# First mixer: input transposed raw, 1/rms put on later as a row, low-rank weights loaded early, first embedding product ahead, values by halves of K

## Chip, cores and metric

One core of one Trainium2 chip runs the whole program in one launch. The metric is device time of an execution in microseconds; for the kernel before it is the median of three runs. TensorE (PE) multiplies, VectorE (DVE) and ScalarE (ACT) do elementwise work, GpSimd (POOL) does small powers and issues some loads, SyncE (SP) issues most loads.

## The reference, cut to what matters

The program is two blocks over 256 positions of width 1024. The first block's first layer is the RWKV mixer, followed by a gated per-layer embedding. The rest (a differential attention layer, feed-forward layers, a Mamba mixer, windowed attention) isn't touched but for where some of its constants are loaded.

```python
def rwkv7_mixer(h, mu, w_in, w0, w1, w2, a0, a1, a2, ...):   # h = rms_norm(x, rw_norm)
    dx = token_shift(h) - h
    xm = h[:, :, None, :] + dx[:, :, None, :] * mu[:4]
    r, k, v, gate = einsum('bsgd,dgc->bsgc', xm, w_in)        # four 1024 x 1024 products
    xw, xa = h + dx * mu[4], h + dx * mu[5]
    w_log = -softplus(-(w0 + tanh(xw @ w1) @ w2)) - 0.5       # low rank, 64
    a = sigmoid(a0 + (xa @ a1) @ a2)                          # low rank, 64
    ...                                                       # recurrence over 256 positions, 16 heads
    return (y * silu(gate)) @ w_out

g = sigmoid(rms_norm(h, pe_norm[i]) @ pe_w_gate[i])
h = h + g * (p[i] @ pe_w_proj[i])                             # i = 0, 1; p[i] is 256 x 256
```

## The kernel before

Weights come from DRAM in f32 tiles of 512 KB or 256 KB (`wload`: tile wr). ScalarE copies a tile to its high part wh, VectorE subtracts to get the low part wl, and each product of f32 accuracy is three matmuls: high by high, high by low, low by high. The activations are split in the same way. Tiles of 128 x 512 come from one pool (`s`, 36 of them); a load into a tile waits until the tile's last reader is done.

The first stage, `rwkv`, runs in this order. x (four tiles of 128 x 512) is squared and summed on ScalarE (`rstd`), GpSimd takes the power -1/2, VectorE scales the four tiles (hn), TensorE transposes them in sixteen 128 x 128 pieces, and ScalarE evacuates them with the gain rw_norm as a column into hT. VectorE makes the differences dx between neighbouring positions. `mixf` makes the mixed input of one projection for two of eight K slices (two multiply-adds on VectorE), `mix` splits it. `value(g)`, `gate(g)`, and the k and r products in `pre(g)` are made for four groups g of 256 columns by `linear2_g`, which yields after every half of a weight tile of four K slices. `lora` makes the two low-rank products from the weights wa, and wm, which is wa times the mu column. Its result feeds the second low-rank product in `pre(g)`, with the weights w2 of that group (tile w in the trace), and with that the recurrence begins.

The code builds its steps as generators, and `weave` runs several in turns. The order on each engine is then set by a scheduler, except that instructions given to `late` stay in program order. Engines work strictly in that order. The last `weave` of the stage runs four streams (one per group: `pre`, `scores`, `solve`, `post`), the gates, and, from step 50 on, `ple_proj(0)` and `ple_proj(1)`: each transposes p[i], multiplies it by pe_w_proj[i] in four groups of twelve matmuls, and stores the product to DRAM (pp) for the stage that adds it.

Loads around it: ScalarE's queue carries the constants, rw_norm, rw_mu, and through the stage the rows (`rows`) and w2 weights of each group. SP carries x, the weights and eleven small vectors (`load_vec`) of later stages. GpSimd carries the level masks lev, wa and five column vectors (`mid_cols`).

Of the kernel before, what the change touches and what calls it, by code (L numbers as in the profile page):

```python
# [18 lines left out]
P = 128  # L19
# [122 lines left out]
class Net:  # L142
    def __init__(self, ctx, tc, I, out, cst, dbg=None):
        self.tc, self.nc, self.I, self.out = tc, tc.nc, I, out
        self.dbg = dbg or {}
        nc = tc.nc
        self.V, self.A, self.T, self.G = nc.vector, nc.scalar, nc.tensor, nc.gpsimd
        self.uid, self.at = 0, None
        en = lambda name, bufs, **k: ctx.enter_context(tc.tile_pool(name=name, bufs=bufs, **k))
        self.cp = en("cp", 1)  # L150
        self.wp = en("wp", 1)
        self.sp = en("sp", 36)
        self.mp = en("mp", 4)
# [42 lines left out]
    def tt(self, out, a, b, op):  # L196
        self.V.tensor_tensor(out=out, in0=a, in1=b, op=op)  # L197

    def mul(self, out, a, b):
        self.tt(out, a, b, ALU.mult)  # L200
# [10 lines left out]
    def ts(self, out, a, s1, op0, s2=None, op1=None):  # L211
        if s2 is None:
            self.V.tensor_scalar(out=out, in0=a, scalar1=s1, scalar2=None, op0=op0)
        else:
            self.V.tensor_scalar(out=out, in0=a, scalar1=s1, scalar2=s2, op0=op0, op1=op1)  # L215
# [6 lines left out]
    def act(self, out, a, f=AF.Copy, **k):  # L222
        self.A.activation(out, a, f, **k)  # L223

    def mm(self, out, l, r, start=True, stop=True):
        self.T.matmul(out, l, r, start=start, stop=stop)  # L226
# [22 lines left out]


    def prologue(self, cst):
# [4 lines left out]
        nc.scalar.dma_start(self.cst, cst[:, :C_KEEP])  # L256
# [35 lines left out]
    def load_x(self, tile, early=False):  # L292

        self.H = {(t, f): tile[:, t * 2 + f] for t in range(2) for f in range(2)}
        for (t, f), h in self.H.items():
# [41 lines left out]
    def wload(self, W, k0, kn, n0, nn):  # L337
# [10 lines left out]
        if self.nw <= 3:  # L348
            self.late(ins)
# [203 lines left out]
    def ple_proj(self, i):  # L553
# [4 lines left out]
        self.nc.sync.dma_start(pv, I["p"][i, 0].rearrange("(t p) d -> p t d", p=P))  # L558
# [47 lines left out]
    def rwkv(self, nxt):  # L606
# [21 lines left out]
        self.G.dma_start(lev[:, :7], self.cdram[:, C_LEV:C_LEV + 7 * P].rearrange("p (a b) -> p a b", a=7))  # L628
# [307 lines left out]
        for q, n in enumerate(("rw_w1", "rw_a1")):  # L936
            self.late(self.G.dma_start(wa[:, :, q], I[n][0].rearrange("(k p) n -> p k n", p=P)))
# [5 lines left out]
        weave(chain(*[value(g) for g in range(4)]), chain(lora(), mix(1, *xk), mix(0, *xr)))  # L943
        weave(mix(3, *xg))
        def residual():
# [9 lines left out]
              after(FP, chain(self.ple_proj(0), self.ple_proj(1))), when(done(OP[0]), after(OP[1], chain(take(l0, OP[2]), take(l1, OP[3])))),  # L955
# [4 lines left out]
    def diff(self, nxt):  # L960
# [7 lines left out]
        for j in range(2):  # L968
            self.mul(lt[:, j * 64:(j + 1) * 64], self.vec[f"da_lq{j + 1}"], self.vec[f"da_lk{j + 1}"])
# [121 lines left out]
    def ssm(self, nxt):  # L1091
# [92 lines left out]
        self.act(ar, self.vec["ssm_a_log_2"], AF.Exp)  # L1184
# [27 lines left out]
        self.ts(hD, self.vec["ssm_d_2"], 0.5, ALU.mult)  # L1212
# [3 lines left out]
        self.ts(mneg, self.tri, 1.0, ALU.subtract, -NEG, ALU.mult)  # L1216
# [344 lines left out]
```

## Time and profile before

| | us |
|---|---|
| three runs | 1552.46, 1554.59, 1555.87; median 1554.59 |
| the profiled execution | 1552.2 |
| its span, first to last instruction | 1550.0 |
| TensorE busy | 1499.0 (97%) |
| VectorE busy | 1063.5 (69%) |
| ScalarE busy | 813.6 (52%) |
| chain that ended last, share on TensorE | 85% |

The span is the time from the first instruction to the last; 2.2 us of the execution's own time lie around it. Busy time of TensorE is counted over pipelined matmuls, so a full TensorE may still have small holes. In a timeline row the first number is the start in us, the second the time that the merged instructions took, x the count, and the bracket the idle time ahead with what ended it. Line numbers are those of the kernel before.

### The profile page before, as it was taken

The numbers are of one execution on the slowest core, as the hardware profiler recorded it, in microseconds if no ns is written. First come the engines' busy times: TensorE is split into PE (matmuls) and PEld (weight loads), VectorE is DVE, ScalarE is ACT, GpSimd is POOL, SyncE is SP. The second block draws the span as 40 slices with busy tenths as digits, with TensorE's granted clock in tenths as the row PEclk, the third lists the DMA queues.
The fourth block names the chain that finished last, engine by engine and source line by source line (L and its number), as shares of the span: only waits on it lengthen the run. The fifth ranks groups of instructions, "written<-read, shape, count | busy, mean of one in ns | idle before, by whom it ended". The sixth has DMA issues, their size and how long they took to land.

```text
span 1550.0 us, 25809 instructions
## 1 busy us (share of the span) xinstructions
PE 1499.0 (97%) x10164; PEld 1336.5 (86%) x10164; DVE 1063.5 (69%) x1798; ACT 813.6 (52%) x1374; POOL 76.7 (5%) x79
## 2 busy tenths in 40 slices
PE   4999999999899999999999999999999999999998
PEld 3988998777678999887788899988999987799987
DVE  6887887787487665559888656655756547766563
ACT  3546556555466543447667644444644445754342
POOL 0000001111101000000000000000000002000000
PEclk9999999999999999999999999999999999999999
DMA  7421324657846654664443655474654753355453
GB/s 208 140 80 59 93 83 137 222 179 148 251 156 192 192 166 151 241 196 130 115 135 110 205 173 167 147 249 149 192 189 133 249 189 109 96 177 177 150 204 109
DMA packets 145501, 249.90 MB, mean 161 GB/s; under 512 B 11161, under 2 KB 42921, under 8 KB 145380
## 3 DMA queue, kind: packets, MB, share of 16 engines
q1 hardware_dynamic: 138420, 233.87, 47.2%
q0 software_dynamic: 3200, 10.81, 3.3%
q10 hardware_dynamic: 3760, 3.58, 0.9%
q8 instruction: 80, 1.31, 0.3%
q14 instruction: 41, 0.34, 0.1%
HBM read 242.16 MB, written 6.29 MB: 160 GB/s over the span
## 4 chain that ended last, share of the span: by engine, by line
PE 85%; DVE 6%; DMA 3%; ACT 2%; POOL 2%; issue 1%; ACTq 0%; POOLq 0%; DVEq 0%
PE pl L226 71%; PE ps L226 10%; PE ps L229 3%; DVE wl L197 1%; DMA wr<-in_da_w_in_dram 1%; DVE s L197 1%; DMA wa<-in_rw_a_dram 1%; DVE s L209 1%; ACT wh L223 1%; ACT s L223 1%; POOL m L234 1%; DMA wr<-in_pe_w_gate_dram 0%; POOL m L1382 0%; ACT e L223 0%; DVE ac L209 0%
## 5 line engine op out<-in xcount | busy, mean ns | idle before, releaser
L226 PE MATMUL pl<-wh,s 128*128 128x512 f32 (+1 forms) x2336 | 678.8, 369 | 5.6 <-DVE s L197 2.9
L197 DVE TENSOR_TENSOR wl<-wr,wh 128x1024 fp32r<-128x1024 f32 (+1 forms) x460 | 528.5, 1173 | 120.9 <-ACT wh L223 119.9
L223 ACT ACTIVATE wh<-wr 128x1024 fp32r<-128x1024 f32 (+1 forms) x460 | 450.9, 1012 | 175.4 <-PE pl L226 105.7
L226 PE MATMUL pl<-s,wh 128*128 128x256 f32 x2816 | 509.1, 283 | 0.0
L226 PEld LDWEIGHTS pl<-wh,s 128*128 128x128 f32 x2336 | 422.8, 190 | 74.7 <-DVE s L197 4.0
L226 PEld LDWEIGHTS pl<-s,wh 128*128 128x128 f32 x2816 | 439.4, 192 | 0.2
L226 PE MATMUL pl<-wl,s 128*128 128x512 f32 (+1 forms) x1168 | 430.5, 369 | 2.0 <-DVE wl L197 2.0
L226 PE MATMUL pl<-s,wl 128*128 128x256 f32 x1408 | 398.5, 283 | 0.0
L226 PEld LDWEIGHTS pl<-s,wl 128*128 128x128 f32 x1408 | 270.2, 192 | 0.0
L226 PEld LDWEIGHTS pl<-wl,s 128*128 128x128 f32 x1168 | 221.7, 190 | 35.4 <-DVE wl L197 3.2
L223 ACT ACTIVATE s<-s 128x512 f32<-128x512 f32 (+2 forms) x97 | 61.0, 629 | 209.6 <-DVE s L197 209.4
L197 DVE TENSOR_TENSOR s<-pl,s 128x512 f32<-128x512 f32 x44 | 30.4, 691 | 93.7 <-PE pl L226 93.7
L197 DVE TENSOR_TENSOR s<-pl,R 128x512 f32<-128x512 f32 x44 | 30.3, 691 | 82.8 <-PE pl L226 82.7
L234 POOL TENSOR_TENSOR m<-m,base 128x2 f32<-128x2 f32 (+2 forms) x25 | 25.3, 1016 | 990.7 <-DVE m L215 990.7
L223 ACT ACTIVATE h<-ps 128x512 f16<-128x512 f32 x88 | 48.3, 601 | 29.3 <-PE ps L226 27.3
L223 ACT ACTIVATE s<-ps,base 128x256 fp32r<-128x256 f32 (+1 forms) x104 | 45.7, 471 | 23.6 <-PE ps L229 12.2
L209 DVE SCALAR_TENSOR_TENSOR s<-ps,base,s 128x256 fp32r<-128x256 f32 x96 | 43.7, 479 | 6.8 <-ACT s L223 5.6
L223 ACT ACTIVATE junk<-H 128x512 bf16<-128x512 f32 x40 | 25.1, 627 | 43.6 <-DVE H L209 29.2
L226 PE MATMUL ps<-h,h 128*128 128x128 f16 x544 | 43.8, 220 | 2.8 <-ACT h L223 2.8
L209 DVE SCALAR_TENSOR_TENSOR s<-s,s 128x512 f32<-128x512 f32 x56 | 38.4, 686 | 10.1 <-ACT s L223 9.4
L226 PEld LDWEIGHTS <-h 128*128 128x128 f16 x576 | 35.6, 99 | 10.7 <-issue 6.0
L209 DVE SCALAR_TENSOR_TENSOR H<-pl,m,H 128x512 f32<-128x512 f32 x16 | 12.0, 751 | 47.1 <-PE pl L226 47.1
(231 smaller groups left out, 1290.1 us busy)
## 6 DMA issues: line engine op xcount, KB each, us to landing
wr<-in_ffn_w_dram SPq DMA_DIRECT2D x248, 512.0 KB, 4.9
wr<-in_ssm_w_in_dram SPq DMA_DIRECT2D x40, 512.0 KB, 4.2
wr<-in_rw_w_in_dram SPq DMA_DIRECT2D x32, 512.0 KB, 4.0
wr<-in_da_w_in_dram SPq DMA_DIRECT2D x32, 512.0 KB, 5.1
wr<-in_pe_w_gate_dram SPq DMA_DIRECT2D x16, 512.0 KB, 6.3
wr<-in_ffn_w_dram SPq DMA_DIRECT2D x32, 256.0 KB, 3.0
wr<-in_ssm_w_out_dram SPq DMA_DIRECT2D x16, 512.0 KB, 3.9
wr<-in_rw_w_out_dram SPq DMA_DIRECT2D x8, 512.0 KB
```

The costliest lines, as they stand in the source:

```text
L197: self.V.tensor_tensor(out=out, in0=a, in1=b, op=op)
L209: self.V.scalar_tensor_tensor(out=out, in0=a, scalar=sc, in1=b, op0=op0, op1=op1, **k)
L223: self.A.activation(out, a, f, **k)
L226: self.T.matmul(out, l, r, start=start, stop=stop)
L229: self.T.transpose(out, a, self.ident)
L234: self.G.tensor_tensor(out=out, in0=out, in1=self.mhalf[:, :out.free_size()].rearrange("p (a b) -> p a b", a=out.shape[1]) if len(out.shap ...
```

## The change

In `rwkv` the scaling by 1/rms is gone. TensorE transposes x itself, ScalarE evacuates with the gain as before, and 1/rms is put on afterwards: the two diagonal matrices dg of 1/rms are multiplied by ones, which gives a row R_ of 1/rms over the positions on all partitions, and VectorE multiplies the four hT tiles by it. `ple_proj(0)` leaves the last weave and runs ahead of that: a first part before the low-rank weights, the rest behind the row, its instructions kept in program order (`pinned`). The low-rank weights come from SP, behind x, p[0] and the first embedding weight; x and wa share memory, so the load waits for the last reader of x. The values run as first halves of K for all four groups, then second halves. Half of the constants, the level masks, the vectors, the rows and the w2 weights go to GpSimd's queue.

```diff
     def prologue(self, cst):
-        nc.scalar.dma_start(self.cst, cst[:, :C_KEEP])
+        nc.scalar.dma_start(self.cst[:, :C_CAUS], cst[:, :C_CAUS])
...
+    @contextmanager
+    def pinned(self):
+        self.pin = True
+        yield
+        self.pin = False
+
+    def kept(self, ins):
+
+        if self.pin:
+            self.late(ins)
+        return ins
...
     def load_vec(self):
         for name, o in self.vec.items():
-            self.nc.sync.dma_start(o, self.bc(self.I[name], o.shape[1]))
+            self.late(self.G.dma_start(o, self.bc(self.I[name], o.shape[1])))
...
     def rwkv(self, nxt):
...
         r = self.rstd()
-        hn = {}
-        for f in range(2):
-            for t in range(2):
-                o = hn[t, f] = b()
-                self.ts(o[:], self.H[t, f], r[:, t:t + 1], ALU.mult)
         for k0 in range(0, 8, 2):
             ps = self.pt()
             for j in range(2):
                 for t in range(2):
-                    k = k0 + j
-                    self.tr(ps[:, j * 256 + t * P:j * 256 + (t + 1) * P], hn[t, k // 4][:, (k % 4) * P:(k % 4 + 1) * P])
-            x, d = hT[k0 // 2], dx[k0 // 2]
+                    self.tr(ps[:, j * 256 + t * P:j * 256 + (t + 1) * P], self.hsrc(t, k0 + j))
             for j in range(2):
-                self.act(x[:, j], ps[:, j * 256:(j + 1) * 256], scale=self.col("rw_norm", k0 + j))
+                self.act(hT[k0 // 2][:, j], ps[:, j * 256:(j + 1) * 256], scale=self.col("rw_norm", k0 + j))
+
+        side = self.ple_proj(0)
+        with self.pinned():
+            weave(take(side, 3))
+        for q, n in enumerate(("rw_w1", "rw_a1")):
+            self.late(nc.sync.dma_start(wa[:, :, q], I[n][0].rearrange("(k p) n -> p k n", p=P)))
+        dg, R_ = b((P, 2, P)), b((P, 256))
+        ps = self.pl()
+        for t in range(2):
+            self.ts(dg[:, t], self.ident, r[:, t:t + 1], ALU.mult)
+            self.mm(ps[:, t * P:(t + 1) * P], self.ones, dg[:, t])
+        self.act(R_[:], ps[:, :256])
+        with self.pinned():
+            weave(side)
+        for x, d in zip(hT, dx):
+            self.mul(x[:], x[:], both(R_[:]))
             self.sub(d[:, :, 1:256], x[:, :, 0:255], x[:, :, 1:256])
             self.ts(d[:, :, 0:1], x[:, :, 0:1], -1.0, ALU.mult)
+        self.late(self.G.dma_start(lev[:, :7], self.cdram[:, C_LEV:C_LEV + 7 * P].rearrange("p (a b) -> p a b", a=7)))
+        self.late(self.G.dma_start(self.cst[:, C_CAUS:], self.cdram[:, C_CAUS:C_KEEP]))
...
-                nc.scalar.dma_start(o[:, j], bass.AP(tensor=a.tensor, offset=a.offset + g * 256, ap=[[0, P], [1, 256]]))
+                ins = self.G.dma_start(o[:, j], bass.AP(tensor=a.tensor, offset=a.offset + g * 256, ap=[[0, P], [1, 256]]))
...
-                nc.scalar.dma_start(w2[at:at + 64, q], I[m][0, :, g * 256:(g + 1) * 256])
-                nc.scalar.dma_start(w2[one:one + 1, q], I[c0][:, g * 256:(g + 1) * 256])
+                for d, w in ((w2[at:at + 64, q], I[m][0]), (w2[one:one + 1, q], I[c0])):
+                    ins = self.G.dma_start(d, w[:, g * 256:(g + 1) * 256])
...
-        for q, n in enumerate(("rw_w1", "rw_a1")):
-            self.late(self.G.dma_start(wa[:, :, q], I[n][0].rearrange("(k p) n -> p k n", p=P)))
...
-        weave(chain(*[value(g) for g in range(4)]), chain(lora(), mix(1, *xk), mix(0, *xr)))
+        vs = [value(g) for g in range(4)]
+        weave(chain(*[take(v, 2) for v in vs], *vs), chain(lora(), mix(1, *xk), mix(0, *xr)))
...
-              after(FP, chain(self.ple_proj(0), self.ple_proj(1))), when(done(OP[0]), after(OP[1], chain(take(l0, OP[2]), take(l1, OP[3])))),
+              after(FP, self.ple_proj(1)), when(done(OP[0]), after(OP[1], chain(take(l0, OP[2]), take(l1, OP[3])))),
```

The scheduler then orders each engine anew. On ScalarE, at the head, the evacuations of the transposes (s from ps) stood before among row loads, and mixed inputs (s from b) followed:

```order
L223 ACTIVATE s_97<-ps_126,base_72 128x256 x2
L709 DMA row_115_582<-in_rw_k_a_dram 128x256
L709 DMA row_115_582<-in_rw_r_k_dram 128x256
L709 DMA row_470_2145<-in_rw_ln_b_dram 128x256
L223 ACTIVATE s_98<-ps_135,base_72 128x256 x2
L709 DMA row_470_2145<-in_rw_ln_w_dram 128x256
L223 ACTIVATE s_99<-ps_144,base_72 128x256 x2
L223 ACTIVATE s_100<-ps_153,base_72 128x256 x2
L223 ACTIVATE s_168<-b_165 128x512
```

Now the last evacuation is followed by the split of p (s_152), the weight copies of the embedding product (wh from wr), the row of 1/rms (b_179) and the evacuations of the four product groups (s from pl):

```order
L223 ACTIVATE s_99<-ps_138,base_72 128x256 x2
L223 ACTIVATE s_152<-ps_147 128x512
L223 ACTIVATE wh_159<-wr_158 128x2x256
L223 ACTIVATE b_179<-pl_180 128x256
L223 ACTIVATE s_186<-pl_157 128x512
L223 ACTIVATE wh_191<-wr_190 128x2x256
L223 ACTIVATE s_208<-pl_189 128x512
L223 ACTIVATE wh_213<-wr_212 128x2x256
L223 ACTIVATE s_230<-pl_211 128x512
L223 ACTIVATE wh_235<-wr_234 128x2x256
L223 ACTIVATE wh_304<-wr_303 128x1024
```

An evacuation of one group and the weight copy of the next alternate from group to group. On VectorE, where the values end, the two first low parts of k (wl_624, wl_654) stood before ahead of the last value group's reduction (L692 from pl_469):

```order
L197 TENSOR_TENSOR s_462<-b_458,s_461 128x512
L197 TENSOR_TENSOR s_467<-pl_376,hold_90 128x512
L209 SCALAR_TENSOR_TENSOR b_555<-s_104,base_72,s_100 128x256
L197 TENSOR_TENSOR wl_624<-wr_622,wh_623 128x1024
L197 TENSOR_TENSOR wl_654<-wr_652,wh_653 128x1024
L692 TENSOR_REDUCE hold_90<-pl_469 128x8
L197 TENSOR_TENSOR wl_697<-wr_695,wh_696 128x1024
```

Now, behind the reduction of the last value group pl_430, which is the row just ahead of these, come the gate's mixed inputs (b and s) and only then the first low part of k, wl_729:

```order
L210 SCALAR_TENSOR_TENSOR b_639<-s_100,base_72,s_96 128x256
L214 TENSOR_SCALAR hold_90<-hold_90 128x8
L210 SCALAR_TENSOR_TENSOR b_646<-s_101,base_72,s_97 128x256
L198 TENSOR_TENSOR s_637<-pl_430,hold_90 128x512
L198 TENSOR_TENSOR s_643<-b_639,s_642 128x512
L210 SCALAR_TENSOR_TENSOR b_646<-s_101,base_72,s_97 128x256
L210 SCALAR_TENSOR_TENSOR b_653<-s_102,base_72,s_98 128x256 x2
L198 TENSOR_TENSOR s_650<-b_646,s_649 128x512
L210 SCALAR_TENSOR_TENSOR b_660<-s_103,base_72,s_99 128x256
L198 TENSOR_TENSOR s_657<-b_653,s_656 128x512
L210 SCALAR_TENSOR_TENSOR b_660<-s_103,base_72,s_99 128x256
L198 TENSOR_TENSOR wl_729<-wr_727,wh_728 128x1024
```

The first low part of k moved from ahead of the last value reduction to twelve steps behind it.

## Rows read from the trace of the kernel before

**Rows 1.** The page: busy time by engine, and TensorE's busy tenths in 40 slices.
```profile
PE 1499.0 (97%) x10164; PEld 1336.5 (86%) x10164; DVE 1063.5 (69%) x1798; ACT 813.6 (52%) x1374; POOL 76.7 (5%) x79
...
PE   4999999999899999999999999999999999999998
```

**Rows 2.** Stretches: length, busy time of each engine, granted clock, DMA share, GB/s.
```profile
25.00:30.00 5.00, 3.72 (x15) 3.53 (x16) 5.00 (x13) 1.89 (x3) 0.00 (x0) 0.50 0.39 113
...
30.00:30.50 0.50, 0.50 (x5) 0.50 (x5) 0.50 (x2) 0.00 (x0) 0.00 (x0) 0.85 0.05 13
```

**Rows 3.** Timeline of the head, 0 to 24 us: first matmul, squares, transposes, evacuations.
```profile
7.55 0.33 PE L309 MATMUL ps<-base,s 56*128 56x56 f32 x1 [7.55 <-DMA s<-in_rw_mu_dram]
...
8.24 0.63 ACT L223 ACTIVATE junk<-x 128x512 bf16<-128x512 f32 x1 [2.32 <-DMA x<-in_x_dram]
...
8.99 0.63 ACT L223 ACTIVATE junk<-x 128x512 bf16<-128x512 f32 x1
...
16.01 3.46 PE L229 MATMUL ps<-base,b 128*128 128x128 f32 x15 [0.23 <-DVE b L213]
...
21.54 1.57 ACT L223 ACTIVATE s<-ps,base 128x256 f32<-128x256 f32 x4 [0.18 <-issue]
```

**Rows 4.** Timeline of VectorE: the wait for the low-rank weights.
```profile
23.52 0.69 DVE L197 TENSOR_TENSOR wa<-wa,base 128x512 f32<-128x512 f32 x1 [3.53 <-DMA wa<-in_rw_w_dram]
```

**Rows 5.** Timeline of TensorE: first products, end of the values, start of the recurrence.
```profile
26.28 1.19 PE L226 MATMUL ps<-s,wa 128*128 128x256 f32 x2 [6.80 <-DMA wa<-in_rw_a_dram]
...
27.70 0.41 PE L226 MATMUL pl<-wh,s 128*128 128x256 f32 x1
27.91 0.41 PE L226 MATMUL pl<-wl,s 128*128 128x256 f32 x1
...
33.15 3.19 PE L226 MATMUL ps<-s,wa 128*128 128x256 f32 x14
...
58.24 0.39 PE L226 MATMUL pl<-wl,s 128*128 128x256 f32 x1
...
71.24 1.94 PE L226 MATMUL ps<-w,hold 65*128 65x256 f32 x8
```

**Rows 6.** Groups by shape, 60 to 330 us: busy and mean ns, idle before.
```profile
L223 ACT ACTIVATE s<-pl 128x512 f32<-128x512 f32 x12 | 7.2, 614 | 3.9 <-PE pl L226 3.9
...
L197 DVE TENSOR_TENSOR wl<-wr,wh 128x512 fp32r<-128x512 f32 x8 | 5.4, 684 | 0.0
...
L223 ACT ACTIVATE wh<-wr 128x512 fp32r<-128x512 f32 x8 | 4.9, 647 | 0.0
```

**Rows 7.** Landing times by line: L937 (wa, GpSimd), L346 (weights, SP), L283 (columns, GpSimd).
```profile
DMA to landing us min/median/max: 8.7/9.6/10.4
...
DMA to landing us min/median/max: 3.6/5.9/9.3
...
DMA to landing us min/median/max: 3.2/3.9/4.2
```

**Rows 8.** Timeline of VectorE: mixing steps, a reduction and a split, two low parts.
```profile
35.03 4.84 DVE L209 SCALAR_TENSOR_TENSOR b<-s,base,s 128x256 f32<-128x256 f32 x12
...
52.70 0.68 DVE L692 TENSOR_REDUCE hold<-pl 128x8 f32<-128x512 f32 x1
53.30 0.68 DVE L197 TENSOR_TENSOR s<-b,s 128x512 fp32r<-128x512 f32 x1
...
56.97 2.35 DVE L197 TENSOR_TENSOR wl<-wr,wh 128x1024 fp32r<-128x1024 f32 x2
```

**Rows 9.** One stretch of the recurrence, columns as in rows 2.
```profile
240.00:260.00 20.00, 17.81 (x209) 16.60 (x208) 13.77 (x26) 14.47 (x29) 2.16 (x4) 1.00 0.46 157
```

**Rows 10.** Timeline of ScalarE, 70 to 280 us: first and last of 27 load issues.
```profile
73.22 0.47 ACTq L720 DMA_DIRECT2D w<-in_rw_w_dram  x1
...
265.73 0.80 ACTq L709 DMA_DIRECT2D row<-in_rw_ln_w_dram  x1
```

**Rows 11.** Timeline of GpSimd: the first of the five column loads.
```profile
58.54 0.55 POOL L283 DMA_DIRECT2D s<-in_da_norm_dram  x1 [41.71 <-PE pl L226]
```

More of the change, by code (lines that the diff above doesn't have):

```diff
@@ L196, in tt @@
     def tt(self, out, a, b, op):
-        self.V.tensor_tensor(out=out, in0=a, in1=b, op=op)
+        return self.kept(self.V.tensor_tensor(out=out, in0=a, in1=b, op=op))
     def mul(self, out, a, b):
-        self.tt(out, a, b, ALU.mult)
+        return self.tt(out, a, b, ALU.mult)
     def add(self, out, a, b):
@@ L212, in ts @@
         if s2 is None:
-            self.V.tensor_scalar(out=out, in0=a, scalar1=s1, scalar2=None, op0=op0)
-        else:
-            self.V.tensor_scalar(out=out, in0=a, scalar1=s1, scalar2=s2, op0=op0, op1=op1)
+            return self.V.tensor_scalar(out=out, in0=a, scalar1=s1, scalar2=None, op0=op0)
+        return self.V.tensor_scalar(out=out, in0=a, scalar1=s1, scalar2=s2, op0=op0, op1=op1)
     def masked(self, out, a, b, least, init=3.0e38):
@@ L222, in act @@
     def act(self, out, a, f=AF.Copy, **k):
-        self.A.activation(out, a, f, **k)
+        return self.kept(self.A.activation(out, a, f, **k))
     def mm(self, out, l, r, start=True, stop=True):
-        self.T.matmul(out, l, r, start=start, stop=stop)
+        self.kept(self.T.matmul(out, l, r, start=start, stop=stop))
     def tr(self, out, a):
@@ L248, in late @@
         self.tc.keep_in_program_order(ins)
+    @contextmanager
+    def pinned(self):
+        self.pin = True
+        yield
+        self.pin = False
+    def kept(self, ins):
+        if self.pin:
+            self.late(ins)
+        return ins
     def prologue(self, cst):
@@ L294, in load_x @@
         self.H = {(t, f): tile[:, t * 2 + f] for t in range(2) for f in range(2)}
-        for (t, f), h in self.H.items():
+        for t, f in ((0, 0), (1, 0), (0, 1), (1, 1)):
+            h = self.H[t, f]
             ins = self.nc.sync.dma_start(h, self.I["x"][0, t * P:(t + 1) * P, f * 512:(f + 1) * 512])
@@ L347, in wload @@
         self.nw = getattr(self, "nw", 0) + 1
-        if self.nw <= 3:
+        if self.nw <= 7:
             self.late(ins)
@@ L557, in ple_proj @@
         pv = p[:].rearrange("p (t d) -> p t d", t=2)
-        self.nc.sync.dma_start(pv, I["p"][i, 0].rearrange("(t p) d -> p t d", p=P))
+        ins = self.nc.sync.dma_start(pv, I["p"][i, 0].rearrange("(t p) d -> p t d", p=P))
+        if i == 0:
+            self.late(ins)
         outs = [([], [])]
@@ L708, in rows @@
                 a = I[n]
-                nc.scalar.dma_start(o[:, j], bass.AP(tensor=a.tensor, offset=a.offset + g * 256, ap=[[0, P], [1, 256]]))
+                ins = self.G.dma_start(o[:, j], bass.AP(tensor=a.tensor, offset=a.offset + g * 256, ap=[[0, P], [1, 256]]))
+                if g == 0:
+                    self.late(ins)
             return o
@@ L719, in pre @@
                 one = 64 if q == 0 else 63
-                nc.scalar.dma_start(w2[at:at + 64, q], I[m][0, :, g * 256:(g + 1) * 256])
-                nc.scalar.dma_start(w2[one:one + 1, q], I[c0][:, g * 256:(g + 1) * 256])
+                for d, w in ((w2[at:at + 64, q], I[m][0]), (w2[one:one + 1, q], I[c0])):
+                    ins = self.G.dma_start(d, w[:, g * 256:(g + 1) * 256])
+                    if g == 0:
+                        self.late(ins)
             for q, o in enumerate((lw, a)):
@@ L968, in diff @@
         for j in range(2):
[L969 removed]
+            self.late(self.mul(lt[:, j * 64:(j + 1) * 64], self.vec[f"da_lq{j + 1}"], self.vec[f"da_lk{j + 1}"]))
         self.V.tensor_reduce(out=ls[:], in_=lt[:, :128].rearrange("p (a c) -> p a c", a=2), axis=AX.X, op=ALU.add)
@@ L1183, in ssm @@
         ar = cut(32)
-        self.act(ar, self.vec["ssm_a_log_2"], AF.Exp)
+        self.late(self.act(ar, self.vec["ssm_a_log_2"], AF.Exp))
         dta = cut(128).rearrange("p (a b c) -> p a b c", a=2, b=2)
@@ L1211, in ssm @@
         hD = cut(32)
-        self.ts(hD, self.vec["ssm_d_2"], 0.5, ALU.mult)
+        self.late(self.ts(hD, self.vec["ssm_d_2"], 0.5, ALU.mult))
         sb = self.m([P, 8, P], BF16, "sb", 1)
@@ L1215, in ssm @@
         self.late(self.V.tensor_copy(idb, self.ident))
-        self.ts(mneg, self.tri, 1.0, ALU.subtract, -NEG, ALU.mult)
+        self.late(self.ts(mneg, self.tri, 1.0, ALU.subtract, -NEG, ALU.mult))
         b8 = lambda ap: ap.unsqueeze(2).broadcast_to([P, 8, 64])
```

1 line of the change is left out of this document (removed).

## The prediction

> **What bounds the kernel now.** I read the page first: TensorE is busy in 97% of the span, and of the 40 slices only the first falls well below the rest [rows 1]. Whatever this change moves, it can win only idle TensorE time at the head, or TensorE work itself. Next the stretches of the head: from 25 to 30 us TensorE's granted clock is 0.50, that is 1.2 GHz, and it comes back to 2.4 GHz within the half microsecond behind 30.0 [rows 2]. Then the timeline of the head, engine by engine. TensorE's first instruction waits to 7.55 us for the row of rw_mu; ScalarE squares x, VectorE scales it by 1/rms, and the sixteen transposes behind that end at 19.5 [rows 3]. VectorE then stands 3.53 us for the low-rank weights [rows 4], and TensorE 6.80 us for the second of them, to 26.28. Behind the low-rank product it runs gapless: values end at 58.2, and 108 products of k and r (48, 48 and 12) bring it to 71.24, where the recurrence's first product starts [rows 5]. 13.0 us for 108 gives 0.12 us each.
>
> So some 22 of the first 26 us are idle on TensorE. Whether the change wins any of it depends on when VectorE, which makes every mixed input and every low weight part, can feed TensorE.
>
> **The change part by part.** The sum is made against the profiled execution's own 1552.2 us (span 1550.0, 2.2 around it), which stands 2.4 under the median 1554.59.
>
> *1. Raw transposes, to the first embedding product.* The four scalings vanish and the transposes no longer wait for 1/rms. They wait for rw_mu's row instead, ahead of them on TensorE. With half the constants and the level masks moved off, I take its landing at 6.0 instead of 7.55. Then 0.33 for the small matmul, four transposes at 0.23 (3.46/15), one evacuation at 0.39 (1.57/4): 7.6 [rows 3]. ScalarE now alternates: three squares at 0.75 and two evacuations, so x is squared by 10.7; five more evacuations to 12.6; then copies of the transposed p 0.61 and of the weight 0.65, and VectorE's low part 0.68 [rows 6]. With hand-offs the first embedding product is complete in its inputs at 14.7. Bounds: 13.9 (rw_mu at 5.2) and 16.3 (still 7.55).
>
> *2. Low-rank weights early.* Their memory is that of x, so SP issues them once x is transposed and squared, at 10.7. VectorE's multiplication of them now stands ahead of the four multiplications by the 1/rms row. Landing times nearby: 3.6 at best, 5.9 in the median for weight tiles on SP, 10.4 at worst for these very weights from GpSimd [rows 7]. I take 5.9, the same queue: 16.6. With 0.69 [rows 4] and four multiplications at 0.60 (52.70 to 53.30) [rows 8] VectorE is free at 19.7. The second embedding weight's high part would be ready at 17.6 (1.6 for eleven matmuls and their tail, 0.61, 0.65), so 2.1 us are lost here; by the ends 0 and 6.6.
>
> The Trainium skill, DMA: Bandwidth & Descriptors, section Issuing engine by pattern, says that loads issued by sync or scalar are generally faster than those from gpsimd. By it this load lands nearer 3.6, the 2.1 us vanish, and the total falls to 1557.2. The rows bear this out only in part, since the slowest SP load of the head (9.3) is about as slow as GpSimd's.
>
> *3. The embedding product leads.* On ScalarE the evacuation of one group stands ahead of the next group's weight copy. So each of groups 2 to 4 is a closed ring: low part, twelve matmuls 1.64, evacuation 0.61, copy 0.65, low part 0.68: 3.6 us, with VectorE's next rows queued behind. The fourth low part ends at 19.7 + 0.7 + 7.1 = 27.5. TensorE is idle over half of each ring; at half clock a matmul takes 0.21 [rows 5], 1.1 more a ring. I add 1.3 (bounds 0 and 3.3): 28.8. Behind it VectorE has 0.4 of waiting, two low parts at 1.14, four differences at 0.67, and two mixing steps at 0.40 [rows 8]: 35.0 for the first mixed input.
>
> *4. Values by halves of K.* Half a product needs only two of the four mixed tiles, which is what keeps TensorE fed from here: 192 x 0.12 = 23.0 and nine low-rank products at 0.456 (3.19/7) [rows 5] make 27.1, and VectorE's list up to the last low part sums to about 24, with 2.9 for its 24 matmuls behind it. Both say 27.3: values end at 62.3, **4.1 later** than 58.2.
>
> *5. Behind the values* a new wait opens. The next matmuls need the first low part of k. On VectorE it now stands behind the reduction of the last value group and twelve steps more: 0.60, seven mixing steps at 0.40, four 512-wide ones at 0.60, a small one at 0.08 and the low part itself, 1.2: 7.1 us in which TensorE has two matmuls. Before, two low parts of k were ready when the values ended (56.97, two in 2.35) [rows 8]. With 90 matmuls then, the recurrence starts 18.0 after the values instead of 13.0: **5.0 later**. The head shows what such an idle stretch costs besides: 6.80 us idle, then 0.21 a matmul from 26.3 to about 30.2 [rows 2, 5], half of those 3.9 us lost: **1.9** (or nothing).
>
> *6. Given back in the recurrence.* The first embedding product no longer runs there: 48 x 0.12 and four transposes, 6.68. But 16 k and r products that stood ahead of its start (108 against 92) now stand behind it, 1.92: **-4.8**. TensorE is nearly full there, so this becomes time. 2.2 us are idle from 240 to 260 [rows 9], which products of w_out, now early enough to fill, can take. 27 row and weight loads leave ScalarE's queue, 11.9 us of issue in all, 0.47 the first and 0.80 the last [rows 10]. For both I take **-1.5** (0 to -4.7).
>
> *7. Small loads on GpSimd.* 23 now follow one another there once a tile is free at the values' end: 5 columns, 11 vectors, 3 rows, 4 weights. At 0.55 each [rows 11] the last is issued 12.6 us later and lands at about 16.5 with the 3.9 of the columns [rows 7], 1.5 ahead of need. Hidden, barely. The masks, casts and the two products with the ones matrix cost nothing: they lie in idle time of their engines.
>
> Sum: 4.1 + 5.0 + 1.9 - 4.8 - 1.5 = +4.7; 1552.2 + 4.7 = 1556.9, and 2.4 for the median: **1559.3 us**.
>
> **The rivals.** *Faster:* rw_mu lands at 5.2 and the low-rank weights in 3.6; no ring runs at half clock. The values then end at 58.1. No clock is lost behind them, and the recurrence returns its idle 2.2 and 2.5 of ScalarE's issue time: -0.1 + 5.0 - 4.8 - 4.7 = -4.6, 1550.0. For it speaks that ScalarE loses 11.9 us of issue; against it, that TensorE and not ScalarE is what runs full. *No change:* full clock throughout and the fast landing, but little more in the recurrence: values at 60.0: 1.8 + 5.0 - 4.8 - 1.5 = +0.5, 1555.1. *Slower still:* GpSimd's chain of loads. If they land as the low-rank weights did (10.4, [rows 7]) and not as the columns, the last is there 23.0 after the values, and the recurrence, due at 18.0, waits 5.0: 1564.3. It decides from a landing of 5.4 on. The Trainium skill's rule that part 2 cites (DMA: Bandwidth & Descriptors, Issuing engine by pattern) speaks for this one, as these loads go from scalar to gpsimd. That the embedding product doesn't lead or the loads don't move is excluded by the order printed above.
>
> **How the numbers follow.** Forecast 0.37, slower still 0.11, no change 0.27, faster 0.25. 0.2% is 3.1 us, about what a measurement can tell from no change: faster 0.25, same 0.27, slower 0.48. The worst ends together (rw_mu 7.55, weights 10.4, half clock) give some 1568, the best 1550. I leave a tenth or less beyond each side: 1550 to 1566. With both signs open, the forecast's own range is 1556 to 1563.
>
> **What would show it.** Right: first transposes near 6 to 7; rings of 3.5 us or more in the embedding product; first mixed input near 35; a hole of 6 to 7 us on TensorE when values end near 62, waiting for VectorE's low part, with a granted clock of 0.50 behind it; recurrence from about 82 instead of 71; then fewer TensorE microseconds up to 290. Wrong: a first mixed input before 30, no hole behind the values, or a gap at the recurrence's start that waits for GpSimd's loads.

## The result and the profile after

The changed kernel takes 1571.55 us in the median of four runs (1569.54 to 1574.28); the kernel before took 1554.13 beside it. The ratio is 1.0112, with a 95% interval of 1.0095 to 1.0128: 17.4 us slower. The forecast was 1559.3, 4.7 us slower, with a range up to 1566. The sign was right, the size was not, and the time lies above the range. The profiled execution has a span of 1567.8 us, against 1550.0.

The page of the changed kernel answers to [rows 1]: busy time by engine, TensorE's busy tenths in 40 slices of 39 us, and its granted clock in tenths.

```profile
PE 1511.2 (96%) x10168; PEld 1342.7 (86%) x10168; DVE 1065.0 (68%) x1800; ACT 814.0 (52%) x1375; POOL 101.3 (6%) x125
...
PE   6899999699899999999999999999999999999998
...
PEclk9899999799999999999999999999999999999999
```

The first slice is fuller than before, as the change means it to be. But slice 8, at 274 to 313 us, is new: busy 0.6 at a clock of 0.7, where the kernel before shows a full slice. That is the end of the stage `rwkv`. Three stretches of the changed kernel show it in numbers (length, busy us of PE, PEld, DVE, ACT and POOL, then granted clock, DMA share and GB/s):

```profile
0.00:82.00 82.00, 60.29 (x400) 56.55 (x400) 57.35 (x111) 36.80 (x60) 18.16 (x37) 0.92 0.68 190
82.00:200.00 118.00, 115.49 (x1015) 102.38 (x1014) 94.09 (x177) 65.43 (x113) 21.07 (x27) 1.00 0.28 72
200.00:325.00 125.00, 112.67 (x930) 96.42 (x929) 93.53 (x172) 63.92 (x115) 13.80 (x16) 0.93 0.36 116
```

The same stretches of the kernel before:

```profile
0.00:82.00 82.00, 59.94 (x410) 55.98 (x411) 61.72 (x122) 37.90 (x63) 8.00 (x14) 0.96 0.56 165
82.00:200.00 118.00, 114.92 (x1059) 102.68 (x1059) 96.80 (x184) 64.39 (x110) 6.54 (x4) 1.00 0.27 83
200.00:325.00 125.00, 120.22 (x960) 105.19 (x957) 98.67 (x176) 75.55 (x139) 13.04 (x16) 1.00 0.46 152
```

In the first 82 us TensorE is idle for 21.7 us after and 22.1 before: the embedding product made there did not come out of the idle time. In the last stretch it is idle for 12.3 us after and 4.8 before, and at a lower clock.

Now the steps in order. TensorE's timeline at the head, answering to [rows 3, 5]: raw transposes, the four groups of the embedding product, the low-rank products.

```profile
6.54 3.67 PE L229 MATMUL ps<-base,x 128*128 128x128 f32 x16
...
18.32 0.39 PE L226 MATMUL pl<-wh,s 128*128 128x256 f32 x1 [0.51 <-ACT wh L223]
...
21.83 0.38 PE L226 MATMUL pl<-wh,s 128*128 128x256 f32 x1 [1.20 <-ACT wh L223]
...
25.32 0.38 PE L226 MATMUL pl<-wh,s 128*128 128x256 f32 x1 [1.20 <-ACT wh L223]
...
29.34 3.72 PE L226 MATMUL ps<-s,wa 128*128 128x256 f32 x16 [1.72 <-DVE s L214]
```

The groups of the embedding product stand 3.5 us apart: the closed ring of the forecast. The low-rank weights, issued by SP at 10.74, landed 3.2 us after their issue (in the kernel before 8.7 to 10.4 from GpSimd, [rows 7]), and VectorE multiplied them at 14.26 without a wait; the 3.53 us of [rows 4] are gone.

The end of the values, the wait behind it and the recurrence's first product, on TensorE, answering to the last two of [rows 5]:

```profile
59.43 0.52 PE L226 MATMUL pl<-wh,s 128*128 128x256 f32 x3
66.88 0.58 PE L226 MATMUL pl<-wl,s 128*128 128x256 f32 x1 [6.93 <-DVE wl L198]
67.25 0.63 PE L226 MATMUL pl<-wh,s 128*128 128x256 f32 x2
...
80.17 1.03 PE L226 MATMUL ps<-w,hold 65*128 65x256 f32 x4
```

The values end at 59.95, 1.7 later than before. Then comes the forecast wait for the first low part of k (which VectorE begins at 65.60), and products at half clock, 0.21 us each, to 72.0. The recurrence starts at 80.17 instead of 71.24: **8.9 us later**. From there the two kernels make the same recurrence, and the changed one should gain. It loses as much again. The four streams' states, on VectorE of the changed kernel (before they were written at 149.71, 192.69, 245.25 and 272.37):

```profile
159.14 0.58 DVE L214 TENSOR_SCALAR S<-ps,hold 64x64 f32<-64x64 f32 x2 [0.25 <-PE ps L226]
...
203.75 0.27 DVE L214 TENSOR_SCALAR S<-ps,hold 64x64 f32<-64x64 f32 x1
...
258.87 0.58 DVE L214 TENSOR_SCALAR S<-ps,hold 64x64 f32<-64x64 f32 x2
...
286.22 0.58 DVE L214 TENSOR_SCALAR S<-ps,hold 64x64 f32<-64x64 f32 x2 [1.93 <-PE ps L226]
```

And TensorE where the third and the fourth stream end; the transposes (L229) of a stream's result open its last products of w_out:

```profile
279.79 0.39 PE L226 MATMUL pl<-wh,s 128*128 128x512 f32 x1
284.44 1.09 PE L229 MATMUL ps<-base,s 128*128 128x128 f32 x4 [4.27 <-DVE s L210]
...
297.95 0.56 PE L226 MATMUL ps<-sa,GB 128*128 128x64 f32 x4
305.77 1.08 PE L229 MATMUL ps<-base,s 128*128 128x128 f32 x4 [7.26 <-DVE s L210]
```

Before, these two waits were 0.96 and 1.48 us:

```profile
270.46 0.63 PE L229 MATMUL ps<-base,s 128*128 128x128 f32 x4 [0.96 <-DVE s L209]
...
281.23 0.56 PE L226 MATMUL ps<-sa,GB 128*128 128x64 f32 x4
...
289.71 0.63 PE L229 MATMUL ps<-base,s 128*128 128x128 f32 x4 [1.48 <-DVE s L209]
```

The first addition to the residual comes at 310.51 instead of 293.10, **17.4 later**, and it stays so to the end of the program. On VectorE, the kernel before first, then the changed one:

```profile
293.10 0.68 DVE L197 TENSOR_TENSOR H<-pl,H 128x512 f32<-128x512 f32 x1
```

```profile
310.51 0.69 DVE L198 TENSOR_TENSOR H<-pl,H 128x512 f32<-128x512 f32 x1 [2.29 <-PE pl L226]
```

What stands on TensorE between the marks tells why. Counted in the order of its instructions, products that don't belong to the recurrence itself (256 wide at 0.12 us: k, r, gates, embedding; 512 wide at 0.23 us: w_out):

| from, to | before: products | us | after: products | us |
|---|---|---|---|---|
| recurrence's start, first state | 220 | 78.5 | 220 | 79.0 |
| first, second state | 154 | 43.0 | 170 | 44.6 |
| second, third state | 142 | 52.6 | 142, and 14 of w_out | 55.1 |
| third, fourth state | 48, and 16 of w_out | 27.1 | 34 of w_out | 27.4 |
| fourth state, last transposes | 52 of w_out | 17.3 | 24 of w_out | 19.6 |
| last transposes, residual | | 3.4 | | 4.7 |
| sum | | 221.9 | | 230.3 |

48 products left the recurrence, and no line is shorter for it. The remaining embedding product slid forward into the first one's place; behind it the scheduler set whatever was ready, products of w_out (SP issues their first weight at 212.3 instead of 226.5, though the streams run 9 us and more later). What is short is what stood last: ahead of the last transposes 24 products of w_out instead of 52. The column shows where the 8.5 us came in: 4.7 up to the third state, 3.8 behind it.

### The profile page after: what moved, and what is told of

It reads as the page before. It is cut to its first block, busy times and chain, and to the rows that moved or that the text cites. A ratio compares the mean times of both kernels' runs of the same rounds, so it can differ in the third digit from the quotient of the medians.

```text
span 1567.8 us, 25827 instructions
## 1 busy us (share of the span) xinstructions
PE 1511.2 (96%) x10168; PEld 1342.7 (86%) x10168; DVE 1065.0 (68%) x1800; ACT 814.0 (52%) x1375; POOL 101.3 (6%) x125
## 4 chain that ended last, share of the span: by engine, by line
PE 84%; DVE 8%; ACT 3%; DMA 2%; POOL 2%; issue 1%; ACTq 0%; POOLq 0%; DVEq 0%
PE pl L226 71%; PE ps L226 10%; PE ps L229 3%; DVE wl L198 2%; DVE s L198 1%; DMA wr<-in_da_w_in_dram 1%; ACT s L223 1%; ACT wh L223 1%; POOL m L234 1%; DVE b L210 1%; DVE ac L210 1%; DVE s L210 1%; ACT e L223 0%; POOL m L1410 0%; POOL s L1024 0%
## 5 line engine op out<-in xcount | busy, mean ns | idle before, releaser
L226 PE MATMUL pl<-wh,s 128*128 128x512 f32 (+1 forms) x2336 | 686.9, 372 | 11.4 <-ACT wh L223 8.0
L226 PEld LDWEIGHTS pl<-wl,s 128*128 128x128 f32 x1168 | 223.3, 191 | 44.1 <-DVE wl L198 12.3
L229 PE MATMUL ps<-base,s 128*128 128x128 f32 x200 | 33.5, 284 | 14.8 <-DVE s L210 11.5
L226 PEld LDWEIGHTS <-h 128*128 128x128 f16 x576 | 35.4, 100 | 10.7 <-issue 5.2
```

Of the source, the lines that this page charges most:

```text
L226: self.kept(self.T.matmul(out, l, r, start=start, stop=stop))
L229: self.T.transpose(out, a, self.ident)
```

## The experiments

The question is which part of the change costs the 17.4 us, and whether the second half is that order of the fill (theory F) or only the late start (theory L). There are twelve kernels. "The stretch" is the time from the recurrence's first product to the first residual addition. The kernel before took 1554.13 us beside the changed kernel, 1553.55 beside experiments 1 to 4, 1553.10 beside 5 to 8 and 1552.29 beside 9 to 12. So where kernels of different groups are compared, a difference of medians is followed, in brackets, by the difference of their distances from the kernel before beside each.

**1. No leading embedding product.** `ple_proj(0)` goes back into the last weave; all else of the change stays.

```diff
-        if i == 0:
-            self.late(ins)
...
-        side = self.ple_proj(0)
-        with self.pinned():
-            weave(take(side, 3))
...
-        with self.pinned():
-            weave(side)
...
-              after(FP, self.ple_proj(1)), when(done(OP[0]), after(OP[1], chain(take(l0, OP[2]), take(l1, OP[3])))),
+              after(FP, chain(self.ple_proj(0), self.ple_proj(1))), when(done(OP[0]), after(OP[1], chain(take(l0, OP[2]), take(l1, OP[3])))),
```

> The changed kernel, but with the first embedding product back in the last weave, where the kernel before has it. From the recurrence's first product to the first residual addition the kernel before takes 221.9 us, the changed one 230.3. Theory F (fill): the freed slots were taken by products of w_out, which then lack at the end of the stage; with the embedding product back, that stretch returns to 222 to 224, the two holes of 4.3 and 7.3 us ahead of the last transposes shrink to 3 us together, and the time falls by about 8 (half clock behind the holes included) and by what the rings cost at the head, some 4 to 6, less the 5 to 6 us that the product then takes again inside the stretch: 1558 to 1563. Theory L (late start): the streams simply began 8.9 us later and their own latency carries that to the end; the stretch stays near 230 whatever fills it, and the time falls only by the head's few us: 1566 to 1569.

Measured: 1552.13 us, ratio to the kernel before 0.9987 (0.9975 to 0.9999). So the leading product alone costs more than the whole change, 19.4 us (18.8), more than either theory had. The recurrence starts at 72.34, 7.8 sooner, and the stretch is 220.3, 10.0 shorter. That is F's sign, 1.7 below its 222 to 224; by L it would have stayed near 230. TensorE at the start of the recurrence and at the last two groups of transposes:

```profile
72.34 1.10 PE L226 MATMUL ps<-w,hold 65*128 65x256 f32 x4 [0.34 <-DMA w<-in_rw_w_dram]
...
270.05 0.63 PE L229 MATMUL ps<-base,s 128*128 128x128 f32 x4 [1.00 <-DVE s L210]
...
289.30 0.63 PE L229 MATMUL ps<-base,s 128*128 128x128 f32 x4 [1.49 <-DVE s L210]
```

**2. Low parts of k ahead of the gate's mixed inputs.** These are made inside the last weave.

```diff
+FM = 12
...
-        weave(mix(3, *xg))
...
-        weave(after(FH, residual()), after(FG[0],
+        weave(after(FH, residual()), after(FM, mix(3, *xg)), after(FG[0],
```

> The changed kernel, but the gate's mixed inputs are made inside the last weave, from its 12th step, so that the low parts of k stand ahead of them on VectorE. If the hole behind the values is VectorE's twelve steps, TensorE's wait of 6.93 us there and the half clock behind it (2.6 us) go, the recurrence starts at 71 to 73 instead of 80.2, and, since the order at the stage's end is unchanged, the two holes there stay and the time falls by 7 to 9: 1562 to 1565. If the weights' landing or their copies on ScalarE set that wait instead, the start stays at 78 or later and the time within 3 us of 1571.5.

Measured: 1566.99 us, ratio 1.0092 (1.0064 to 1.0119): 4.6 (4.0) less than the changed kernel, half of what was expected. The 6.93 us are gone, so they were VectorE's twelve steps. But 43 more products of k and r now stand ahead of the recurrence (5.2 us), which starts at 75.78 and not at 71 to 73, and TensorE is short of work later: 111.27 us busy in the middle stretch against 115.49. The waits at the stage's end are unchanged, 11.5 us in two.

```profile
82.00:200.00 118.00, 111.27 (x972) 97.72 (x971) 97.02 (x186) 64.28 (x112) 18.99 (x23) 0.97 0.29 77
```

**3. Products of w_out held back.** They are kept in program order, behind the third stream.

```diff
+    def held(self, gen):
+
+        while True:
+            self.pin = True
+            try:
+                next(gen)
+            except StopIteration:
+                return
+            finally:
+                self.pin = False
+            yield
...
-              after(FP, self.ple_proj(1)), when(done(OP[0]), after(OP[1], chain(take(l0, OP[2]), take(l1, OP[3])))),
+              after(FP, self.ple_proj(1)), when(done(OP[0]), after(OP[1], self.held(chain(take(l0, OP[2]), take(l1, OP[3]))))),
```

> The changed kernel, but the sixty early products of w_out are kept in program order, so that they stand behind the third stream's end and not ahead of it: none ahead of the last but one group of transposes, 15 between the last stream's last product and its transposes (0 in the changed kernel), 39 instead of 18 behind them. Theory F: the streams no longer queue behind w_out products, some 36 of 0.23 us or 8 us, the holes at the end are filled, and the time falls by 6 to 11: 1560 to 1565. Theory L: the streams' latency sets their end, which stays at 305 for the last transposes; 21 more products then stand behind it, 4.8 us: 1573 to 1577.

Measured: 1570.17 us, ratio 1.0107 (1.0084 to 1.0129): 1.4 us (0.8) under the changed kernel, within the noise, and neither theory's time. The transposes of the third stream come 8.6 us sooner (275.86, of which 1.0 is the start), as F has it: the streams did queue behind w_out. The rest then fell to the fourth stream, whose steps now stand behind blocks of 6 to 16 held products, and to 39 products behind its transposes; the first residual addition comes at 313.04, 2.5 us later than in the changed kernel. TensorE at the two groups of transposes:

```profile
275.86 1.08 PE L229 MATMUL ps<-base,s 128*128 128x128 f32 x4 [2.57 <-DVE s L210]
...
304.16 0.63 PE L229 MATMUL ps<-base,s 128*128 128x128 f32 x4 [2.15 <-DVE s L210]
```

**4. The kernel before without its first embedding product.** The stage that adds it reads the second one.

```diff
-        scr = self.pps[i]
+        scr = self.pps[1]
...
-              after(FP, chain(self.ple_proj(0), self.ple_proj(1))), when(done(OP[0]), after(OP[1], chain(take(l0, OP[2]), take(l1, OP[3])))),
+              after(FP, self.ple_proj(1)), when(done(OP[0]), after(OP[1], chain(take(l0, OP[2]), take(l1, OP[3])))),
```

> The kernel before without its first embedding product: the stage that adds it reads the second one instead, so 48 products of 0.12 us and four transposes, 6.7 us of TensorE, are left out and nothing takes their place at the head. The forecast's sixth step (freed work becomes time) expects 6.7 to 8 us less: 1546 to 1548, and no hole at the end of the stage. Theory F expects the order at the stage's end that the changed kernel has: holes of 8 to 12 us in all ahead of the last two groups of transposes, half clock behind them, and a time within 3 us of the kernel before, 1552 to 1558, though it does less.

Measured: 1560.62 us, ratio 1.0043 (1.0031 to 1.0056). It does 6.7 us less on TensorE and takes 7.1 us longer, more than F had. The change leaves the head's code alone: the recurrence starts at 70.05, and the stretch is 228.8 instead of 221.9. The waits for the last two groups of transposes are those of the changed kernel:

```profile
274.05 0.63 PE L229 MATMUL ps<-base,s 128*128 128x128 f32 x4 [4.27 <-DVE s L209]
...
294.08 1.09 PE L229 MATMUL ps<-base,s 128*128 128x128 f32 x4 [7.23 <-DVE s L209]
```

This alone rules out the forecast's sixth step, and L, by which the stretch would have stayed: the recurrence starts no later here than before, and the stretch is 6.9 longer.

**5. The embedding product twice.** The changed kernel makes it at the head, and once more, to no use, where the kernel before has it.

```diff
-    def ple_proj(self, i):
+    def ple_proj(self, i, at=0):
...
-        if i == 0:
+        if i + at == 0:
...
-              after(FP, self.ple_proj(1)), when(done(OP[0]), after(OP[1], chain(take(l0, OP[2]), take(l1, OP[3])))),
+              after(FP, chain(self.ple_proj(0, 2), self.ple_proj(1))), when(done(OP[0]), after(OP[1], chain(take(l0, OP[2]), take(l1, OP[3])))),
```

> The changed kernel, but the first embedding product is made a second time in the last weave, where the kernel before makes it: 48 products and four transposes more, 6.7 us of TensorE, redundant work. The order at the stage's end is then that of the kernel before (28 products of w_out between the last stream's last product and its transposes, 16 ahead of the third stream's). Theory F (fill, and an order in which w_out no longer stands ahead of the third stream): the stretch from the recurrence's first product to the first residual addition, 230.3 us in the changed kernel, falls to 220 to 223 as in the first experiment, the waits ahead of the last two groups of transposes fall from 11.5 to about 2.5 us, and the time falls although there is more work: 1561 to 1565. If work is what counts there, the time rises by 6.7: 1576 to 1580. If only the streams' own latency counts, it stays: 1569 to 1574.

Measured: 1563.83 us, ratio 1.0062 (1.0045 to 1.0079): 6.7 us more work, 7.7 us (6.7) less time than the changed kernel. The stretch is 224.0 instead of 230.3 (1.0 above the range expected), though the recurrence starts 2.2 us later, at 82.42; TensorE's wait for the streams' results from 200 to 325 us (total, times, longest) is that of the kernel before:

```profile
PE ps L229 <- DVE s L210: 2.4, 2, 1.5
```

**9. The second embedding product later.** One number of the changed kernel: it begins at step 62 of the last weave.

```diff
-FH, FG, FP, OP = 70, (30, 2), 50, (6, 0, 4, 6)
+FH, FG, FP, OP = 70, (30, 2), 62, (6, 0, 4, 6)
```

> The changed kernel with one number altered: the remaining embedding product begins at step 62 of the last weave instead of 50, where its fill stood when the first one ran ahead of it. No work is added or taken. In the order 28 products of w_out stand again between the last stream's last product and its transposes, and few ahead of the third stream's. If the loss of the second half is the order of the fill, the waits ahead of the last two groups of transposes fall from 11.5 to 2 to 4 us and the time by 8 to 13: 1558 to 1563. If it was the redundant work of the fifth experiment as such that helped (by keeping the clock up, or by holding the streams apart), the time stays within 3 us of 1571.5.

Measured: 1564.56 us, ratio 1.0081 (1.0065 to 1.0096): 7.0 us (5.2) less than the changed kernel, with the same work. The stretch is 224.1, 6.2 shorter, and of the two waits only the last is left:

```profile
303.67 0.63 PE L229 MATMUL ps<-base,s 128*128 128x128 f32 x4 [1.50 <-DVE s L210]
```

So it is the order, not the redundant work as such. The gain is smaller than expected (the time is 1.6 above the range). Two things go against it: in the profiled execution the recurrence starts 2.8 us later, at 82.96 (the head ran at half clock there, as the last section shows), and some of the idle time moved ahead of the end: TensorE is idle for 8.1 of the last 125 us (12.3 in the changed kernel, 4.8 before).

```profile
200.00:325.00 125.00, 116.92 (x974) 102.65 (x973) 98.42 (x181) 67.25 (x121) 13.34 (x17) 0.97 0.40 129
```

The other runs ask what the rest of the change is worth, without the leading product.

**6. Without it, and low parts of k first** (the edits of 1 and 2 together).

> The first experiment's kernel (no leading embedding product), and the gate's mixed inputs inside the last weave, so that the low parts of k stand ahead of them. In that experiment TensorE is idle for some 7 of the 20 us from 40 to 60 and waits 4.9 us behind the values. If that wait is again VectorE's twelve steps, the recurrence starts 2 to 5 us sooner than 72.3 (it then waits for the w2 loads on GpSimd, which were just in time), and the time falls from 1552.1 to 1547 to 1550. If the order's other moves take it back, as they took half of it in the second experiment (43 products more ahead of the recurrence), 1550 to 1553.

Measured: 1552.81 us, ratio 0.9996 (0.9987 to 1.0006). The recurrence starts 4.5 us sooner, at 67.88, but its first state is 1.7 later (149.64 against 147.96): TensorE's idle time moved behind the start, as in the second experiment.

```profile
82.00:200.00 118.00, 112.83 (x1005) 99.16 (x1004) 97.28 (x187) 64.05 (x110) 15.35 (x18) 0.96 0.27 72
```

**7. Without it, and the values whole.**

```diff
-        weave(chain(*[take(v, 2) for v in vs], *vs), chain(lora()
+        weave(chain(*vs), chain(lora()
```

> The first experiment's kernel with the values made whole, group by group, as in the kernel before. If the halves of K are what keeps TensorE fed at the head, TensorE waits more between 20 and 45 us, the values end 3 to 5 us later and the time rises to 1555 to 1557; if VectorE's mixed inputs limit that stretch in either order, the time stays within 2 us of 1552.

Measured: 1550.07 us, ratio 0.9978 (0.9967 to 0.9988): 2.1 us (1.6) *less* than with halves, against the expected rise; the intervals of the two ratios overlap. In the first 82 us TensorE is idle for 15.1 us, against 17.9 in the first experiment's kernel, whose row is the second here. But the first state comes 2.6 us later (150.53) and only the second is sooner (190.28 against 192.55):

```profile
0.00:82.00 82.00, 66.94 (x447) 61.78 (x448) 62.33 (x119) 39.58 (x63) 17.80 (x37) 0.94 0.64 175
```

```profile
0.00:82.00 82.00, 64.15 (x403) 57.89 (x403) 61.27 (x118) 37.97 (x62) 18.90 (x37) 0.92 0.63 169
```

**8. Without it, and the small loads back** on ScalarE and SP.

```diff
-            self.late(self.G.dma_start(o, self.bc(self.I[name], o.shape[1])))
+            self.nc.sync.dma_start(o, self.bc(self.I[name], o.shape[1]))
...
-                ins = self.G.dma_start(o[:, j], bass.AP(...))
-                if g == 0:
-                    self.late(ins)
+                nc.scalar.dma_start(o[:, j], bass.AP(...))
...
-                    ins = self.G.dma_start(d, w[:, g * 256:(g + 1) * 256])
-                    if g == 0:
-                        self.late(ins)
+                    nc.scalar.dma_start(d, w[:, g * 256:(g + 1) * 256])
```

> The first experiment's kernel with the rows and w2 weights issued by ScalarE and the eleven vectors by SyncE again, as in the kernel before. If ScalarE's issue time (27 loads, 11.9 us) was worth something in the recurrence, the time rises by 1 to 3 us to 1553 to 1555; if GpSimd's row of loads holds the recurrence's start (a wait of 0.34 us for a w2 load was seen there), the start moves ahead by up to 3 us and the time falls to 1549 to 1551; if both are hidden, it stays within 1 us of 1552.

Measured: 1551.81 us, ratio 0.9991 (0.9982 to 1.0000): no difference from 1552.13. The recurrence's first product moved to 65.55, 6.8 us ahead, whether for the loads or for the order that the scheduler then chose; but TensorE only did the same things in another order, and the first state came at 148.77 (147.96 with the loads on GpSimd).

**10. Second embedding product later, values whole** (the edits of 9 and 7).

> The ninth experiment's kernel with the values made whole, group by group. If halves of K cost 2 us behind a leading embedding product as they did without one (seventh against first experiment), 1556 to 1561. If they help there, as the forecast's fourth step had it, since VectorE is further behind, the time rises by 2 to 4: 1560 to 1567.

Measured: 1562.17 us, ratio 1.0067 (1.0052 to 1.0082). That is 2.4 us less than with halves (experiment 9), and the intervals overlap again.

**11 and 12. Without the leading product, values whole:** with low parts of k first (the edits of 1, 7 and 2), and with the small loads back (1, 7 and 8).

> The seventh experiment's kernel (no leading product, whole values), and the gate's mixed inputs inside the last weave. In the sixth experiment that moved the idle time from the head into the recurrence and changed nothing. If it does the same here, 1549 to 1552; if whole values leave VectorE enough room, the idle 15 us of the first 62 shrink by 2 to 4 and the time falls to 1546 to 1548.

> The seventh experiment's kernel with the rows and w2 weights back on ScalarE and the vectors back on SyncE. In the eighth experiment that was worth nothing (within 1 us). Expected the same here: 1549 to 1551. If GpSimd's row of loads held the recurrence's start at 73.4 us, it moves ahead to some 68 and the time falls to 1547 or less.

Measured: 1553.25 us (ratio 1.0008, 0.9998 to 1.0018), 3 us (4.0) worse than the seventh and outside both cases expected; and 1547.45 us (ratio 0.9969, 0.9956 to 0.9982), 0.4 above what the second case asked for, with the start at 67.70. The last is the fastest of all: 4.8 us under the kernel before, and 2.6 us (1.8) under the seventh, whose interval it overlaps; its first state comes 5.2 us sooner (145.31). Of the change it keeps the raw transposes, the row of 1/rms, the early low-rank weights, and the masks and half of the constants on GpSimd. Its first stretch:

```profile
0.00:82.00 82.00, 64.76 (x417) 58.48 (x418) 64.33 (x124) 39.08 (x64) 6.37 (x13) 0.98 0.60 173
```

## Why the forecast was wrong

*Step 1 held.* Transposes at 6.54, x squared by 10.7; the first embedding product had its inputs at 14.3 (14.7).

*Step 2 was too dear.* The low-rank weights landed in 3.2 us, not 5.9, so nothing was lost (2.1 in the sum). The rule that the prediction cited (the Trainium skill, DMA: Bandwidth & Descriptors, Issuing engine by pattern: sync generally faster than gpsimd) would have been nearer here than the median of the queue's weight tiles. The load also moved from 14.7 to 10.7 us, so it isn't shown that the queue alone made it faster.

*Step 3 held.* Rings of 3.5 us (3.6). With the faster landing and one ring at half clock the first mixed input is there at some 32 instead of 35.

*Step 4.* Values end at 59.95 (62.3): the 2.4 us are those of steps 2 and 3. But its claim that halves of K keep TensorE fed isn't borne out. Measured from the kernel before beside each, whole values are faster by 1.6, 2.4 and 3.5 us in three pairs (7 against 1, 10 against 9, 12 against 8) and slower by 1.3 in the fourth (11 against 6); the intervals overlap in all but the third, where they touch, so that whole values are better isn't clearly shown either.

*Step 5 held, and closely.* The wait was 6.93 us (7.1), and from the end of the values to the recurrence's start 20.2 (18.0 and 1.9). At this point the forecast stood at 11.0 us late, the trace at 8.9.

*Step 6 failed, and with it the forecast.* "TensorE is nearly full there, so this becomes time", a gain of 4.8, and 1.5 more from idle slots and ScalarE's queue. Measured: a loss of 8.5, so the term was off by 14.8. Two things were wrong in it. First, the full engine didn't give back the work that was taken from it: the scheduler filled the slots with the next work that was ready. That was the other embedding product and then w_out, ahead of the third stream's last steps (4.7 us up to the third state, in the table above). Second, that work was the cover of the stage's end. There each stream waits for its own steps on VectorE and ScalarE: from the last product of the fourth stream to its transposes it is 7.9 us before, with w_out in between, and 7.3 after, without it. With 28 products in that gap TensorE waited 1.48 us, with none 7.26. The prediction noted that products of w_out would be early enough to fill; it counted that as a gain and didn't ask what would be left for the end. Experiment 4 shows this step by itself, at +7.1 us; 5 and 9 undo it in two ways, at -7.7 (-6.7) and -7.0 (-5.2).

*Step 7 was too tight.* GpSimd's loads waited for the landing of earlier ones (0.71, 1.75 and 2.03 us in the changed kernel), and the recurrence's first product waited 0.34 and 0.87 us for a w2 load in experiments 1 and 5. With halves of K it cost nothing to speak of (experiment 8); with whole values the loads' place may be worth 1.8 us (12 against 7, intervals overlapping). For the changed kernel itself it wasn't tried.

The rival that named slower still gave 1564.3, by the GpSimd loads: the wrong mechanism, and still 7 us short. None of the cases had the end of the stage in it, and so the range, which took in every unknown of the head, didn't reach the time.

What the leading product does at the head is then plain, if not by what mechanism in each piece: the recurrence starts 7.8 us later than without it (its first state 11.2), for 6.7 us of work moved, so it won none of the idle time. Of the 19.4 us between the changed kernel and experiment 1, 7.8 are there, 10.0 in the stretch; the rest is the difference of medians and profiled executions.

Left open: whether whole values feed TensorE better than halves, and why; and whether a place at the head exists where the embedding product would fill idle time; that wasn't tried.

## What to carry to other kernels

When you move work out of a full stage, ask not only what it cost there but what it covered: list what stands on the engine in the last few microseconds of the stage, ahead of the step that everything waits for, and what will stand there once the scheduler has filled the gap with the next ready work. The order of the changed kernel told this before any run: 0 products instead of 28 ahead of the last transposes. The start of a chain is a poor mark too: in experiments 6 and 8 it moved ahead by 4.5 and 6.8 us, and the chain's first result came 1.7 and 0.8 us later.

## What the runs showed of the hardware

Each new hole cost more than its length: behind the waits of 6.93, 4.27 and 7.26 us TensorE's granted clock was at about half, 1.2 GHz, for the next 5 to 7 us. Stretches of the changed kernel around them:

```profile
66.00:72.00 6.00, 5.12 (x24) 5.13 (x25) 3.69 (x4) 2.24 (x3) 3.53 (x7) 0.50 0.93 111
284.00:291.00 7.00, 6.56 (x37) 4.83 (x38) 3.32 (x8) 0.66 (x2) 0.00 (x0) 0.53 0.00 0
305.00:311.00 6.00, 4.54 (x12) 3.45 (x13) 1.81 (x3) 0.60 (x1) 0.00 (x0) 0.50 0.02 7
```

The forecast had counted 1.9 us for the first of them; the other two came with the end of the stage.

And the same order of instructions at the head ran at either clock. In the profiled executions of the changed kernel and of experiments 2 and 3 the stretch behind the last ring had the full clock; in those of experiments 5 and 9, whose head is the same, it had half, and the recurrence started 2.2 and 2.8 us later (82.42 and 82.96). The changed kernel first, then experiment 9:

```profile
28.00:30.00 2.00, 0.66 (x3) 0.60 (x4) 2.00 (x6) 1.21 (x2) 1.45 (x3) 1.00 0.89 247
30.00:32.00 2.00, 2.00 (x11) 1.77 (x10) 2.00 (x7) 0.00 (x0) 0.18 (x1) 1.00 0.72 202
```

```profile
28.00:30.00 2.00, 1.66 (x8) 1.36 (x7) 2.00 (x3) 0.36 (x2) 0.00 (x0) 0.50 0.94 250
30.00:32.00 2.00, 1.76 (x4) 1.50 (x5) 2.00 (x7) 1.24 (x2) 1.41 (x3) 0.50 0.88 254
```

TensorE had been idle for 1.2 us ahead of each of the last two rings in both. What made the clock fall in one execution and not in the other isn't shown; but a single profile can flatter such a head by some microseconds. The profiled execution of the changed kernel is the fastest of its four (1569.54 us, median 1571.55).
